# An encoder layer in split precision: weight loads at their place in the program, and the products by sevens one pair later

## The chip, the core and the metric

The kernel runs on one core of one Trainium2 chip. A core has five engines that each work through a list of instructions of their own: TensorE (PE in the profile; its weight loads are PEld), VectorE (DVE), ScalarE (ACT), GpSimd (POOL) and SyncE (SP), which here only sends transfers. They wait for each other by semaphores. Transfers between the main memory and the on-chip memory (SBUF) run on 16 DMA engines. Matmuls write to PSUM, eight banks in all, of which the program uses four as accumulators ("g") and four for other purposes (x, y, sc0, sc1).

The metric is the device time of one execution in microseconds (us), lower is better. The kernel before took 1131.32 us (median of three runs, 1131.21 to 1131.83).

## What is computed

One layer of a bidirectional encoder over 256 tokens of 2048 features: a norm, one projection to nine groups of 2048 columns, two branches (a gated linear recurrence over 16 heads and a short convolution), an output projection over both branches, a gate, and a last norm.

```python
def reference(x, p, norm_w, w_in, ..., w_out, w_ple, w_ple_gate, final_norm_w):
    h = x
    ...
        hn = _rmsnorm(h, norm_w[i])
        proj = hn @ w_in[i]
        q, v, f_fwd, f_bwd, z_a, b_gate, c_gate, h_b, z_b = jnp.split(proj, IN_SPLITS, axis=-1)
        o_a = _hgrn2_bidirectional(jax.nn.silu(q), v, f_fwd, f_bwd, lb_all[:, i])
        o_a = _head_rmsnorm(o_a, hgrn_norm_w[i]) * jax.nn.silu(z_a)
        y_b = b_gate * _short_conv(c_gate * h_b, conv_w[i])
        o_b = _rmsnorm(y_b, conv_norm_w[i]) * jax.nn.silu(z_b)
        h = h + jnp.concatenate([o_a, o_b], axis=-1) @ w_out[i]
        gate = jax.nn.sigmoid(h @ w_ple_gate[i])
        h = h + (p[i] @ w_ple[i]) * gate
    return _rmsnorm(h, final_norm_w)
```

All of it is in float32, and the weights (some 200 MB) are read once.

## The kernel before

**Split precision.** Each float32 operand of the large products is split into a rounded part and the rest. ACT makes the rounded part by a copy (L103, the "cast"), DVE subtracts it from the raw one (L104, the "split"). A product then takes three matmuls: rounded by rounded, rounded by rest, rest by rounded. The activations are split once; the weights are split as they stream in.

**The stream of weights.** The class `Stream` brings the weights in order. A raw tile holds 2048 columns (1 MB) and has three buffers; it is loaded by SP in `load` (L82). It is used in parts of 1024 columns (or less), and each part has one of five split buffers. `get(i)` opens all parts up to three ahead of part i: `open` takes a split buffer, loads the raw tile if it is not there, and returns what `split` works on. In `get` all of this stands under `high_priority(offset=300)`.

**The planner.** The program is written in order, and a planner in the framework sets the order of each engine's list: of the instructions that are ready it takes the one with the lowest number, and numbers follow the order of the program. `high_priority(offset=300)` lowers the number of what stands under it by 300, so that it comes ahead of up to 300 instructions that stand before it. Only the opening stage has an order by hand for ACT, DVE and PE.

**Ticks.** Work that goes beside the products is queued by `at(dt, fn)`: `tick()` is called behind each k-tile of a product, and `fn` is written into the program when `dt` ticks have passed.

**The stages,** with their lines:

- The opening stage, from 0 to about 40 us: x is split (`x_split`, L286 and L287, which read the tile xf), and the first three products (two forget gates and q) run together over k.
- Heads in pairs, four times two pairs. `gemm_in` makes products of 16 k-tiles with four matmuls each (L344, L346), `evac` takes them out of PSUM (L378, L379), `gemm_two` makes v and z for two pairs (L365 to L367). Beside them run the recurrences: `mix_forgets`, `mix_pair`, `scores` (L543, L587), `outputs`.
- The norm of x is needed late, since a row's scale can be multiplied in behind the product. For it the token rows of x are loaded once more into xf, in two transfers (`load_tokens`, L298, ticks 2 and 3 behind the opening stage), squared and summed (`x_squares`, L305 on ACT and L306 on DVE, ticks 6 to 9, into PSUM banks x and y), turned into scales (`x_norms`, L312 to L316, tick 11) and spread by a product (`norms_spread`, L321 and L322, tick 14). `by_norms` (L383) multiplies the forget gates and q by them; the first pair's gates are mixed at tick 15. The first scores are written at tick 18 of the product of v, and their last operand is dd (L515).
- The convolution branch, eight times four products, up to about 844 us. Behind its last product `turn` (L471 to L475) transposes the last two head pairs through PSUM banks y and x into mixa, the input of the output projection. The residual rows hh are loaded by SP (L773).
- The output projection, 845 to about 1019 us: two column halves u, and for each first the recurrence's branch (mixa), then the convolution's (mixb). Each of these four runs of `half` goes over 16 k-tiles in eight pairs. A pair is normally eight products of 128 x 128 by 512 (two k-tiles, two row blocks, two column blocks), 24 matmuls. Two of the pairs are done by seven products, as in Strassen's scheme, 21 matmuls: they need sums of weight blocks, made on DVE in place in the raw tile (`sums`, L69, L71, L72), and sums of activation blocks (`act_sums`, L685 to L690). `SUMS` says which pairs. Their parts are named singles, single, pairs and more, and the last two come behind sums. Four accumulators beside the main four take the products that go to several outputs (epa in banks x, y, sc0, sc1 for mixa, epb in the "g" banks for mixb); they are taken at the first pair of sevens and emptied at the second.
- The gate, the embedding and the last norm, up to the end. The inputs pr and fw are loaded by SP (L910, L915).

Of the kernel before, what the change touches and what calls it, by code (L numbers as in the profile page):

```python
# [12 lines left out]
ALU = mybir.AluOpType  # L13
# [14 lines left out]
class Stream:  # L28
# [11 lines left out]
    def add(self, *srcs):  # L40


        j = len(self.todo)
        _, k, n = srcs[0].shape
        n *= len(srcs)
        self.todo.append((srcs, k, n))
        first = len(self.where)
        self.where += [(j, h) for h in range(k * n // 1024)]
        return list(range(first, len(self.where)))
# [10 lines left out]
    def sums(self, j, h):  # L60

        b = self.raws[j].rearrange("p (b n) -> p b n", b=4)
        add = self.nc.vector.tensor_tensor
        if h == "singles":
            return b[:, 0:2]
        if h == "single":
            return b[:, 3:4]
        if h == "pairs":
            add(out=b[:, 0:3:2], in0=b[:, 0:3:2], in1=b[:, 2:4], op=ALU.add)  # L69
            return b[:, 0:3:2]  # L70
        add(out=b[:, 3], in0=b[:, 0], in1=b[:, 3], op=ALU.add)  # L71
        add(out=b[:, 1], in0=b[:, 3], in1=b[:, 1], op=ALU.add)  # L72
        return b[:, 1:4:2]

    def load(self, j, k0=0, k1=None, pool=None):
# [30 lines left out]
    def get(self, i):  # L106
        while self.next <= min(i + self.ahead, len(self.where) - 1):
            if self.next not in self.parts:

                with self.tc.high_priority(offset=300):  # L110
                    self.split(*self.open(self.next))
            self.next += 1
        return self.parts[i]

# [2 lines left out]
def tile_hymba_encoder(  # L117
# [45 lines left out]
        for c in (B_CG, B_HB, B_BG, B_ZB):  # L163
            blocks[c, i] = sum((ws.add(w_in[c + i, h]) for h in range(2)), [])

    SUMS = (2, 5)
    oblocks = []
    for u in range(2):
        srcs = [[w_out[2 * u + n, q // 2, :, 2 * (q % 2) : 2 * (q % 2) + 2] for n in range(2)] for q in range(16)]
        oblocks.append([(ws.add_sums if q % 8 in SUMS else ws.add)(*srcs[q]) for q in range(16)])  # L170
    gblocks, pblocks = [], []
# [59 lines left out]
    for j in range(4):  # L231
        sgn = 1 if j < 2 else -1
        pool.affine_select(
            out=tri[:, j, :], in_=tri[:, j, :], compare_op=ALU.is_ge, fill=0.0, base=0,
# [447 lines left out]
    def act_sums(src, dst, a, s):  # L682


        dve.tensor_tensor(out=a, in0=src[:, :, 0], in1=src[:, :, 1], op=ALU.add)  # L685
        a11, a21, a12, a22 = (a[:, k, m * P : (m + 1) * P] for k in range(2) for m in range(2))
        for o, x, y in ((0, a21, a22), (1, a21, a11), (2, a11, s[:, 0]), (3, a12, s[:, 2])):
            dve.tensor_tensor(out=s[:, o], in0=x, in1=y, op=ALU.subtract)
        act.copy(out=dst[:, :, 0], in_=s)
        dve.tensor_tensor(out=dst[:, :, 1], in0=s, in1=dst[:, :, 0], op=ALU.subtract)  # L690
# [10 lines left out]
    for i in range(8):  # L701
# [7 lines left out]
        for m in range(2):  # L709
            ct = 2 * i + m  # L710
            dve.tensor_scalar(cg[:, m, :], u[:, m, 0:T], cvw[:, 0, ct : ct + 1], None, op0=ALU.mult)
            for j in (1, 2):
                dve.scalar_tensor_tensor(
                    out=cg[:, m, :], in0=u[:, m, j : j + T], scalar=cvw[:, j, ct : ct + 1],
                    in1=cg[:, m, :], op0=ALU.mult, op1=ALU.add,
# [10 lines left out]
        for m in range(2):  # L726
            ct = 2 * i + m
            dve.scalar_tensor_tensor(
                out=hb[:, m, :], in0=hb[:, m, :], scalar=cnw[:, ct : ct + 1], in1=sz[:, m, :],
# [13 lines left out]
        if i in (4, 5):  # L743
            a = bp.tile([P, 2, T], F32, tag="sa", name=f"sa{i}")
            b = bp.tile([P, 4, P], F32, tag="sb", name=f"sb{i}")
            k = 2 * SUMS[i - 4]
            act_sums(mixa[:, k : k + 2], suma[:, i - 4], a, b)
# [46 lines left out]
    def three(acc, al, ah, w, start, stop):  # L794
# [3 lines left out]
        pe.matmul(acc, lhsT=al, rhs=w[:, 0], start=False, stop=stop)  # L798

    def half(main, extra, parts, src, sums):  # L800


        banks = None
        for q, ids in enumerate(parts):
# [10 lines left out]
            if banks is None:  # L815
                banks = extra()
            z = SUMS.index(q)
            st, sp = z == 0, z == len(SUMS) - 1

# [51 lines left out]
    for u in range(2):  # L871
        cs = [slice(512 * (2 * u + n), 512 * (2 * u + n + 1)) for n in range(2)]
        for src, sums, main, other, scale in ((mixa, suma, psg, psm, False), (mixb, sumb, psm, psg, True)):
            name = f"p{'ab'[scale]}{u}"
            acc = four(main, name)
            parts = oblocks[u][8 * scale : 8 * scale + 8]
            if u == 0 and not scale:
                for z in range(2):
                    k = 2 * SUMS[z]
                    act_sums(  # L880
                        mixb[:, k : k + 2], sumb[:, z], tmp[:, 0:1].rearrange("p b (k t) -> p (b k) t", k=2),
                        tmp[:, 1:2].rearrange("p b (o t) -> p (b o) t", o=4),
                    )
            for q1, q5, q7, q6 in half([acc[0:2], acc[2:4]], lambda: four(other, "e" + name), parts, src, sums):
                d, v, d7, v7 = (tmp[:, b] for b in range(4))
                add_h(0, cs[0], q1, scale)
                act.copy(out=d, in_=q1)
                dve.tensor_tensor(out=d, in0=d, in1=q6, op=ALU.subtract)
                dve.tensor_tensor(out=v, in0=q5, in1=d, op=ALU.subtract)
                dve.tensor_tensor(out=d7, in0=d, in1=q7, op=ALU.subtract)  # L890
                dve.tensor_tensor(out=v7, in0=v, in1=q7, op=ALU.add)
                add_h(0, cs[1], v, scale)
                add_h(1, cs[0], d7, scale)
                add_h(1, cs[1], v7, scale)
            with tc.high_priority(offset=200):
                for m in range(2):
                    for n in range(2):
                        add_h(m, cs[n], acc[2 * m + n], scale)
        for z in range(2):
            at(5 + 2 * z, lambda u=u, z=z: h_transposed(u, z))  # L900
# [161 lines left out]
```

## Time and profile before

| | us |
|---|---|
| median of three runs | 1131.32 |
| the profiled execution | 1129.86 |
| its span, first to last instruction | 1128.1 |
| PE busy | 1113.0 |
| DVE busy | 785.0 |
| ACT busy | 646.9 |

The rest of the page bears on how the transfers stand. The second part cuts the span into 40 slices of 28 us; a digit is a share in tenths.

```profile
DVE  7689467865966587867665566566668888886664
ACT  6688566755865587564454444444545454455563
PEclk9999999999999999999999999999999999999999
DMA  9744455454546545545555555555556575566542
...
q1 hardware_dynamic: 41616, 212.88, 54.9%
```

The DMA engines are near their limit only in the first slice and busy by half later. DVE is busiest in the slices from 840 to 1010 us, those of the output projection. The granted clock of TensorE (PEclk) stands at full speed in all slices at this grain; single dips show only in a finer table.

How the views are read: a row of a timeline gives start, duration, engine, line, operation and tiles, in brackets the idle time before it and who ended it. A row of the list of waits gives the total, the number of times and the longest. A row of groups gives count, total and the mean in ns. A row of the table of stretches gives the busy time and count of PE, PEld, DVE, ACT and POOL, then the granted clock, the share of the DMA engines and GB/s.

### The profile page before, as it was taken

Reading aid. Unit: us, or ns where it says so; the run is one execution under the profiler, and the core shown is the slowest. Engines: PE = TensorE matmul, PEld = TensorE weight load, DVE = VectorE, ACT = ScalarE, POOL = GpSimd, SP = SyncE. Lnnn points to the kernel's source line nnn. Section 1 sums busy time; section 2 is a strip of 40 time slices with the busy share of each in tenths; the row PEclk is TensorE's granted clock in tenths of the full one; section 3 lists DMA queues with packets and bytes.
Section 4 is the critical chain, followed back from the end, with each engine's and each line's share of the span. In section 5 each row is a group of like instructions: output and inputs, shape, how many; then the busy total and the mean of one; then the engine's idle time right before and its main releaser. Section 6 shows DMA issues by size and latency. Waiting matters only on the chain.

```text
span 1128.1 us, 16505 instructions
## 1 busy us (share of the span) xinstructions
PE 1113.0 (99%) x6506; PEld 956.2 (85%) x6506; DVE 785.0 (70%) x1016; ACT 646.9 (57%) x893; POOL 214.4 (19%) x167
## 2 busy tenths in 40 slices
PE   9998999999999999999999999999999999999997
PEld 8887888888888888888888888888887888888886
DVE  7689467865966587867665566566668888886664
ACT  6688566755865587564454444444545454455563
POOL 1035116210432035211111121111211000000012
PEclk9999999999999999999999999999999999999999
DMA  9744455454546545545555555555556575566542
GB/s 351 286 150 170 167 182 192 140 197 167 178 145 220 168 168 187 177 160 196 182 204 195 192 188 187 186 186 187 192 189 216 188 237 172 186 227 234 202 168 75
DMA packets 41981, 214.27 MB, mean 190 GB/s; under 512 B 4656, under 2 KB 5040, under 8 KB 26288
## 3 DMA queue, kind: packets, MB, share of 16 engines
q1 hardware_dynamic: 41616, 212.88, 54.9%
q8 instruction: 51, 0.84, 0.3%
q10 hardware_dynamic: 288, 0.34, 0.1%
q14 instruction: 26, 0.21, 0.1%
HBM read 211.11 MB, written 2.10 MB: 189 GB/s over the span
## 4 chain that ended last, share of the span: by engine, by line
PE 95%; DVE 2%; ACT 1%; POOL 1%; issue 0%; DMA 0%; DVEq 0%; ACTq 0%; POOLq 0%
PE a L346 36%; PE a L344 18%; PE a L367 5%; PE a L366 5%; PE a L365 5%; PE pg L790 3%; PE pg L789 3%; PE pg L791 3%; PE pa L798 2%; PE pa L797 2%; PE pa L796 2%; PE pb_sc L798 1%; PE pb_sc L797 1%; PE pb_sc L796 1%; PE scps L543 1%; DVE spl L104 1%
## 5 line engine op out<-in xcount | busy, mean ns | idle before, releaser
L104 DVE TENSOR_TENSOR spl<-raw,spl 128x1024 fp32r<-128x1024 f32 (+2 forms) x414 | 510.2, 1242 | 250.2 <-ACT spl L103 249.2
L346 PE MATMUL a<-xs,spl 128*128 128x512 f32 x1792 | 620.6, 394 | 0.5 <-DVE xs L287 0.5
L103 ACT CAST spl<-raw 128x1024 fp32r<-128x1024 f32 (+2 forms) x414 | 415.8, 1011 | 313.0 <-PE a L344 171.1
L344 PE MATMUL a<-xs,spl 128*128 128x256 f32 x1792 | 493.3, 278 | 0.0
L346 PEld LDWEIGHTS a<-xs,spl 128*128 128x128 f32 x1792 | 335.0, 188 | 77.5 <-ACT spl L103 0.7
L344 PEld LDWEIGHTS a<-xs,spl 128*128 128x128 f32 x1792 | 335.9, 188 | 1.9
L365 PE MATMUL a<-spl,xs 128*128 128x512 f32 x256 | 100.7, 393 | 0.0
L367 PE MATMUL a<-spl,xs 128*128 128x512 f32 x256 | 99.8, 390 | 0.0
L366 PE MATMUL a<-spl,xs 128*128 128x512 f32 x256 | 99.7, 389 | 0.0
L378 ACT COPY r<-a 128x256 f32<-128x256 f32 x112 | 40.9, 368 | 53.1 <-PE a L344 53.0
L939 POOL TENSOR_TENSOR hh<-hh,fw 128x512 f32<-128x512 f32 (+1 forms) x9 | 11.3, 1263 | 257.5 <-ACT gt L938 254.9
L367 PEld LDWEIGHTS a<-spl,xs 128*128 128x128 f32 x256 | 48.1, 188 | 10.1
L365 PEld LDWEIGHTS a<-spl,xs 128*128 128x128 f32 x256 | 48.1, 188 | 9.6
L366 PEld LDWEIGHTS a<-spl,xs 128*128 128x128 f32 x256 | 48.1, 188 | 9.4
L789 PE MATMUL pg<-spl,ht 128*128 128x512 f32 (+1 forms) x120 | 45.2, 377 | 0.0
L790 PE MATMUL pg<-spl,ht 128*128 128x512 f32 (+1 forms) x120 | 45.1, 375 | 0.0
L791 PE MATMUL pg<-spl,ht 128*128 128x512 f32 (+1 forms) x120 | 45.0, 375 | 0.0
L383 POOL TENSOR_TENSOR xf<-xf,rbc 128x1024 f32<-128x1024 f32 x8 | 20.4, 2556 | 123.1 <-DVE xf L379 117.8
L524 POOL TENSOR_TENSOR qc<-pf,ge 128x256 f32<-128x256 f32 x16 | 32.8, 2051 | 50.2 <-DVE pf L516 29.2
L796 PE MATMUL pa<-spl,mixa 128*128 128x512 f32 x104 | 40.7, 392 | 0.0
L798 PE MATMUL pa<-spl,mixa 128*128 128x512 f32 x104 | 40.5, 389 | 0.0
L797 PE MATMUL pa<-spl,mixa 128*128 128x512 f32 x104 | 40.5, 389 | 0.0
(266 smaller groups left out, 1270.5 us busy)
## 6 DMA issues: line engine op xcount, KB each, us to landing
raw<-in_w_in_dram SPq DMA_DIRECT2D x106, 1024.0 KB, 4.9
raw<-in_w_in_dram SPq DMA_DIRECT2D x74, 512.0 KB, 4.9
raw<-in_w_out_dram SPq DMA_DIRECT2D x64, 512.0 KB, 5.0
raw<-in_w_gate_dram SPq DMA_DIRECT2D x12, 1024.0 KB, 5.0
raw<-in_w_gate_end_dram SPq DMA_DIRECT2D x8, 512.0 KB, 4.9
xf<-in_xtok_dram SPq DMA_DIRECT2D x2, 1024.0 KB, 6.9
hh<-in_xtok_dram SPq DMA_DIRECT2D x1, 2048.0 KB, 11.1
raw<-in_w_ple_dram SPq DMA_DIRECT2D x4, 512.0 KB, 3.6
```

The lines of the kernel that those rows point to most:

```text
L103: self.nc.scalar.copy(out=v[:, :, 0], in_=r)
L104: self.nc.vector.tensor_tensor(out=v[:, :, 1], in0=r, in1=v[:, :, 0], op=ALU.subtract)
L344: pe.matmul(a[:, :T], lhsT=lhsT, rhs=xs[:, kt, 0, :], start=False, stop=(kt == NKT - 1))
L346: pe.matmul(a, lhsT=lhsT, rhs=xs[:, kt, :, :].rearrange("p s n -> p (s n)"), start=(kt == 0), stop=False)
L365: pe.matmul(acc[m], lhsT=lh, rhs=w[:, kt % 2, 0, :], start=(kt == 0), stop=False)
L366: pe.matmul(acc[m], lhsT=lh, rhs=w[:, kt % 2, 1, :], start=False, stop=False)
L367: pe.matmul(acc[m], lhsT=ll, rhs=w[:, kt % 2, 0, :], start=False, stop=(kt == NKT - 1))
L789: pe.matmul(acc[m], lhsT=lh, rhs=wh, start=(kt == 0), stop=False)
L790: pe.matmul(acc[m], lhsT=lh, rhs=wl, start=False, stop=False)
L791: pe.matmul(acc[m], lhsT=ll, rhs=wh, start=False, stop=(kt == nk - 1))
L796: pe.matmul(acc, lhsT=ah, rhs=w[:, 0], start=start, stop=False)
L797: pe.matmul(acc, lhsT=ah, rhs=w[:, 1], start=False, stop=False)
```

## The change

Two edits. First, `get` calls `open`, and with it `load`, before the block of `high_priority`; only the casts and splits stand under it. The sums in `sums`, which `open` calls, get a block of their own with the same offset. So the loads of the weights (and the requests for tiles) take their numbers from where they stand in the program.

Second, `SUMS` goes from (2, 5) to (3, 5): in each run of `half` the fourth and the sixth pair of k-tiles are done by seven products, and no longer the third and the sixth. The weights' order in memory stays; the sums of activation blocks are those of the fourth pair (heads 6 and 7).

```diff
         b = self.raws[j].rearrange("p (b n) -> p b n", b=4)
-        add = self.nc.vector.tensor_tensor
+
+        def add(out, in0, in1):
+            with self.tc.high_priority(offset=300):
+                self.nc.vector.tensor_tensor(out=out, in0=in0, in1=in1, op=ALU.add)
+
         if h == "singles":
             return b[:, 0:2]
         if h == "single":
             return b[:, 3:4]
         if h == "pairs":
-            add(out=b[:, 0:3:2], in0=b[:, 0:3:2], in1=b[:, 2:4], op=ALU.add)
+            add(out=b[:, 0:3:2], in0=b[:, 0:3:2], in1=b[:, 2:4])
             return b[:, 0:3:2]
-        add(out=b[:, 3], in0=b[:, 0], in1=b[:, 3], op=ALU.add)
-        add(out=b[:, 1], in0=b[:, 3], in1=b[:, 1], op=ALU.add)
+        add(out=b[:, 3], in0=b[:, 0], in1=b[:, 3])
+        add(out=b[:, 1], in0=b[:, 3], in1=b[:, 1])
         return b[:, 1:4:2]
...
             if self.next not in self.parts:
+                part = self.open(self.next)
 
                 with self.tc.high_priority(offset=300):
-                    self.split(*self.open(self.next))
+                    self.split(*part)
             self.next += 1
         return self.parts[i]
...
-    SUMS = (2, 5)
+    SUMS = (3, 5)
```

## The prediction

> **What bounds the kernel now.** I read the page's busy shares first, then the list of waits for PE alone, then a table of stretches.
>
> ```profile
> span 1128.1 us, 16505 instructions
> PE 1113.0 (99%) x6506; PEld 956.2 (85%) x6506; DVE 785.0 (70%) x1016; ACT 646.9 (57%) x893; POOL 214.4 (19%) x167
> ...
> PE scps L543 <- DVE dd L515: 2.9, 1, 2.9
> PE epa_x L796 <- DVE mixa L475: 2.3, 1, 2.3
> ...
> 95.00:845.00 750.00, 750.00 (x4700) 651.08 (x4692) 501.79 (x642) 432.19 (x605) 177.73 (x125) 1.00 0.53 181
> 1120.00:1128.10 8.10, 0.00 (x0) 0.00 (x0) 3.23 (x10) 2.77 (x5) 0.72 (x1) 0.74 0.65 243
> ```
>
> PE is idle 1128.1 - 1113.0 = 15.1 us in all. Of this 8.1 us lie behind the last matmul. Two single waits, the longest of the list, make 5.2: 2.9 us before the first scores (L543) and 2.3 us before the first of the seven products (L796 into epa_x). The rest, under 2 us, lies at the very start. Between 95 and 845 us PE has no idle time at all. So a change that leaves the number of matmuls alone can win only at these two places, and it loses only where it makes PE wait anew. This change leaves the number alone: each half still has two pairs of k-tiles with seven products and six with eight. The two places in the timeline of PE, and what DVE did there:
>
> ```profile
> 856.70 0.39 PE L796 MATMUL pa<-spl,mixa 128*128 128x512 f32 x1
> 859.43 0.47 PE L796 MATMUL epa_x<-spl,mixa 128*128 128x512 f32 x1 [2.34 <-DVE mixa L475]
> ...
> 858.81 0.47 DVE L475 SCALAR_TENSOR_TENSOR mixa<-ogt,vec,mixa 128x256 fp32r<-128x256 f32 x1
> ...
> 89.51 0.39 PE L367 MATMUL a<-spl,xs 128*128 128x512 f32 x1
> 89.74 0.39 PE L365 MATMUL a<-spl,xs 128*128 128x512 f32 x1
> 93.04 0.34 PE L543 MATMUL scps<-qc,dd 128*32 128x128 f32 x2 [2.92 <-DVE dd L515]
> 96.80 0.48 PE L366 MATMUL a<-spl,xs 128*128 128x512 f32 x1
> ...
> 114.88 0.30 PE L543 MATMUL scps<-qc,dd 128*32 128x128 f32 x2
> 117.38 0.40 PE L366 MATMUL a<-spl,xs 128*128 128x512 f32 x1
> ...
> 93.50:94.00 0.50, 0.50 (x30) 0.50 (x26) 0.00 (x0) 0.50 (x2) 0.42 (x2) 0.50 0.00 0
> 857.00:859.50 2.50, 0.16 (x2) 0.10 (x1) 2.50 (x7) 2.35 (x4) 0.00 (x0) 1.00 0.00 0
> ```
>
> A matmul of 512 columns normally starts 0.23 us after the one before (89.51, 89.74). The gap 856.70 to 859.43 is 2.73 us, so this wait costs **2.50**. The gap 89.74 to 93.04 is 3.30 us, so that one costs **3.07**. It has an aftermath: behind it the granted clock is 0.50. The same work, from the first scores to the L366 behind them, takes 96.80 - 93.04 = 3.76 us here and 117.38 - 114.88 = 2.50 us in the next group: **1.26** more. Behind the other wait the clock stays at 1.00.
>
> The Trainium skill (TensorE: Matmul & The Clock Gate, Part 1) says that the array falls to half rate after an idle window of about 3.4 us, that this window runs freely, and that it takes as long a busy one to come back. The trace agrees as far as it goes: half clock behind 2.9 idle us, none behind 2.3. By that rule alone, a shorter wait at the scores would cost its own length without the 1.26; this is a rival below.
>
> **The sevens moved from the third to the fourth pair.** epa_x takes the PSUM bank x, which the last transposed head pair still holds until the L475 above has read it, at 859.28. With the third pair done plainly, PE first has 24 more matmuls (two k-tiles, four accumulators, three each): 24 x 0.227 = 5.4 us. It comes to epa_x at about 856.93 + 5.4 = 862.4 instead of 856.93. L475 then has 3 us to spare. DVE does not do more before that point: the third pair's sums and four splits give way to two splits. Even if the last L475 slipped behind two more splits of 1.3 us it would end at 861.9. I take the whole 2.50 as gained; the bounds are 0 and 2.50.
>
> What the move costs is DVE's, since a pair of sevens is cheap for PE and dear for DVE:
>
> ```profile
> L104 DVE TENSOR_TENSOR spl<-raw,spl 128x1024 fp32r<-128x1024 f32 x380 | 489.0, 1295 | 247.4 <-ACT spl L103 246.4
> L104 DVE TENSOR_TENSOR spl<-raw,spl 128x512 fp32r<-128x512 f32 x30 | 19.6, 685 | 2.8 <-ACT spl L103 2.8
> L69 DVE TENSOR_TENSOR raw<-raw 128x1024 f32<-128x1024 f32 x8 | 9.7, 1218 | 0.1
> L72 DVE TENSOR_TENSOR raw<-raw 128x512 f32<-128x512 f32 x8 | 6.2, 777 | 0.2
> L71 DVE TENSOR_TENSOR raw<-raw 128x512 f32<-128x512 f32 x8 | 5.5, 690 | 0.2
> ...
> 918.66 3.51 DVE L104 TENSOR_TENSOR spl<-raw,spl 128x1024 fp32r<-128x1024 f32 x3
> ...
> 921.87 0.39 PE L796 MATMUL pb_x<-spl,mixb 128*128 128x512 f32 x1
> ```
>
> Sevens: 3 x 1.295 + 0.685 + 1.218 + 0.690 + 0.777 = 7.26 us of DVE in 21 x 0.227 = 4.77 us of PE. A plain pair: 2.59 in 5.45. Fourth, fifth and sixth together: DVE 17.1, PE 15.0, so DVE falls 2.1 us behind in each of the four halves, and two plain pairs no longer lie between. What carries it is work made ahead. Five split buffers let DVE run four parts ahead of PE. The tightest part today is the plain one right behind the sevens: its split starts at 918.66 and lasts about 1.2, PE wants it at 921.87, so 2.0 us are left.
>
> I walk through the new order with PE at the first of the fourth pair as 0. The release of the buffer five parts back starts a cast (1.05), and the split (1.22) follows it. The fifth pair's two parts are ready at 2.5 and 3.9, wanted at 4.8 and 7.5. The sixth pair's parts, with its sums between them, are ready at about 5.1, 5.8, 9.6 and 10.8, wanted at 10.2, 11.6, 12.3 and 13.6. The seventh pair's first is ready at 12.8, wanted at 15.0. The least reserve stays near 2 us, so I take 0. If the reserve were not there, the second sevens would run at DVE's pace: 7.26 - 4.77 = 2.5 us in each half, 10 us in all; that is the other bound.
>
> **The weight loads without precedence.** SP sends nothing but loads until the end, and every weight load waits for its raw buffer. Without precedence a load can only lose its place to another load that is ready: the token rows (L298), the residual rows (L773), the two small ones of the last stage. The place where that matters is the start:
>
> ```profile
> 28.19 0.87 DVE L287 SCALAR_TENSOR_TENSOR xs<-xf,vec,xs 128x256 fp32r<-128x256 f32 x2
> ...
> 13.51 27.01 SPq L82 DMA_DIRECT2D raw<-in_w_in_dram  x8
> 40.57 0.42 SPq L298 DMA_DIRECT2D xf<-in_xtok_dram  x1
> 45.85 0.33 SPq L82 DMA_DIRECT2D raw<-in_w_in_dram  x1
> 46.23 0.42 SPq L298 DMA_DIRECT2D xf<-in_xtok_dram  x1
> ...
> 845.06 0.42 SPq L773 DMA_DIRECT2D hh<-in_xtok_dram  x1
> ...
> 42.91 0.42 DVE L379 TENSOR_TENSOR qt<-a,r 128x256 f32<-128x256 f32 x1
> 54.56 0.69 DVE L306 SCALAR_TENSOR_TENSOR xk<-xf 128x512 f32<-128x512 f32 x1
> 65.72 0.42 DVE L322 COPY rbc<-rps 128x256 f32<-128x256 f32 x1
> 91.15 1.75 DVE L515 TENSOR_TENSOR dd<-xf,dd 128x512 f32<-128x512 f32 x1
> ...
> xf<-in_xtok_dram SPq DMA_DIRECT2D x2, 1024.0 KB, 6.9
> ...
> 74.75 0.39 PE L365 MATMUL a<-spl,xs 128*128 128x512 f32 x1
> ```
>
> The token rows overwrite xf, whose last reader ends at 28.19 + 0.87 = 29.06. Yet they are sent at 40.57 and 46.23, each right behind a weight load. In the program they stand at ticks 2 and 3 of the first product behind the opening stage; the weight loads opened at ticks 12 and 20 were sent before the first of them, and that of tick 28 before the second. So the precedence did hold them back. The whole chain to the late scores hangs on the second: sent 46.23, landed about 53.1, squares from 54.56, norms spread at 65.72, last operand of the scores at 91.15 + 1.75 = 92.90.
>
> Without precedence both should go ahead of the loads of ticks 12 to 28, between 29.1 and 41.0. That brings the second 5 to 17 us forward. The gain is capped, because its squares need a PSUM bank that q's accumulator leaves only with the L379 of 42.91: 54.56 to 43.4, 11 us at most. The scores' own place is tick 18 of the product that starts at 74.75: 54 matmuls, 74.75 + 12.3 = 87.0. The operand must be ready by then, 5.9 us sooner than 92.90. With a move of 5 a wait of about 1 us remains, with 11 none. I take none, since the free time of xf (29.06) lies 17 us back: gain 3.07 + 1.26 = **4.33**, bounds 0 and 4.33.
>
> What the moved transfers cost the weights:
>
> ```profile
> 51.99 1.05 ACT L103 CAST spl<-raw 128x1024 fp32r<-128x1024 f32 x1
> ...
> raw<-in_w_in_dram SPq DMA_DIRECT2D x106, 1024.0 KB, 4.9
> ...
> 88.00:90.00 2.00, 2.00 (x10) 1.43 (x8) 2.00 (x5) 1.98 (x2) 1.63 (x2) 1.00 1.00 397
> ```
>
> At 397 GB/s a token load of 1 MB holds the transfers for 2.6 us, both for 5.3. The load sent at 40.2 (last of the eight) lands after 4.9 us and is first cast at 51.99: 6.9 us to spare. So it is hidden. Uncovered, it would cost up to 5.3 us once. The residual rows (845.06) may pass the weight load sent beside them, which is that of the fifth pair; 2 MB are 5.3 us, and PE comes to that pair only four pairs later, over 20 us. The splits and the sums keep their precedence, and the other moved call, the request for the tiles, issues nothing. These I cost at 0, with 5.3 as the bound if the cover were gone.
>
> **The sum.** 2.50 + 4.33 = 6.83 us. The profiled execution took 1129.86 us (span 1128.1), which gives 1123.0. It was 1.46 under the median of the runs, so on the median: 1131.32 - 6.83 = **1124.5**.
>
> **The rivals.**
> (a) *The order of the loads stays.* SP sends the token rows where it did and the scores wait as before: 1131.32 - 2.50 = 1128.8. For it: nothing in the trace shows why SP did not send them soon after 29 us, when they were free to go. Against it: the three weight loads of later ticks that passed them.
> (b) *The wait at the scores shrinks but stays.* The chain comes 5 us forward, or DVE and ACT, both busy nearly all of 60 to 95 us, give part of it back. About 1.5 us are left and the clock holds, as behind 2.3 idle us: 1126.0.
> (c) *The bank wait comes back one pair later.* The last L475 slips behind the splits past 862.4, the scores gain: 1131.32 - 4.33 = 1127.0.
> (d) *DVE becomes the bound around the fifth pair.* This one ends slower. It decides once more than 2 us of other DVE work (squares of sums, transposes, additions to hh) fall into the 15 us from the fourth to the sixth pair: then each half pays up to 2.5, 1124.5 + 10 = 1134.5. For it: DVE is busy 25 of 27 us in the first half. Against it: that other work has no precedence and can be late.
> (e) *Neither wait goes*: 1131.3.
>
> ```profile
> 863.00:890.00 27.00, 27.00 (x121) 22.37 (x120) 25.19 (x33) 14.04 (x15) 0.00 (x0) 1.00 0.69 237
> ```
>
> **How the numbers follow.** Forecast 0.40, (a) 0.22, (b) 0.15, (c) 0.06, (d) 0.11, (e) 0.06. About 0.2%, 2.26 us, is what a measurement of this kernel can tell from no change. The forecast, (b) and (c) lie clearly beyond it; (a) is 0.22% and falls beyond it in 0.14 of its 0.22. Faster 0.40 + 0.15 + 0.06 + 0.14 = 0.75, same 0.08 + 0.06 = 0.14, slower 0.11. The range reaches from 1123.0 (the sum on the profiled execution itself) to 1129.5 (case (a) with the 0.6 us by which the three runs differ), and leaves out (d) and (e), 0.17.
>
> **What would show it.** Right: the list of waits for PE keeps only the two at the start; L298 is sent before 41 us and rbc copied before 61; the granted clock stays 1.00 from 90 to 97; DVE's last L475 ends before epa_x starts. Wrong: L298 still behind the same weight loads; a wait of PE on a split between the fourth and seventh pair of any half; a cast in 35 to 60 us that waits for a weight transfer.

## The result, and the profile after

| | before | after |
|---|---|---|
| median, us | 1131.26 (1130.22 to 1131.83, 4 runs) | 1122.49 (1121.94 to 1123.00, 4 runs) |
| profiled execution, us | 1129.86 | 1121.94 |
| its span, us | 1128.1 | 1120.2 |

The ratio is 0.9923, with a 95% interval of 0.9906 to 0.9941: faster by 8.8 us. The forecast was 1124.5 with a range from 1123.0 to 1129.5. The sign and both places were right; the time lies 0.5 us below the range.

In the kernel after, lines from L82 on stand four to five lower: the load is L86, cast and split L107 and L108, `load_tokens` L303, the scores L548, `turn`'s last operation L480, the products by sevens L801 to L803, and all sums of weight blocks L66.

The page of after, and the list of waits for PE:

```profile
span 1120.2 us, 16504 instructions
PE 1110.8 (99%) x6506; PEld 955.9 (85%) x6506; DVE 788.6 (70%) x1016; ACT 644.7 (58%) x892; POOL 216.5 (19%) x167
...
PE wps L221 <- DVE wz L216: 1.1, 1, 1.1
```

PE makes the same 6506 matmuls. Its two long waits are gone from the list, and no new one has come; only the opening one is left. DVE has the same 1016 operations. The work is the same; only idle time of PE, and half-clock time behind it, went.

SP's own timeline of after shows how the first wait went (transfers of one line that follow each other are one row, with their count at its end):

```profile
19.94 9.30 SPq L303 DMA_DIRECT2D xf<-in_xtok_dram  x2
29.28 94.90 SPq L86 DMA_DIRECT2D raw<-in_w_in_dram  x25
```

The two token loads, sent at 40.57 and 46.23 before, now stand one behind the other, and the next weight load is behind both. The group begins at 19.94 and ends at 29.24 (19.94 + 9.30). The first load fills the half of xf that was read first; SP sent the second at 28.91, as soon as the last reader of the other half had ended (28.87 in DVE's timeline). From there the timelines of DVE and PE of after show the chain to the scores and, further down, the bank x:

```profile
41.20 0.70 DVE L311 SCALAR_TENSOR_TENSOR xk<-xf 128x512 f32<-128x512 f32 x1
52.30 0.42 DVE L327 COPY rbc<-rps 128x256 f32<-128x256 f32 x1
79.68 0.68 DVE L520 TENSOR_TENSOR dd<-xf,dd 128x512 f32<-128x512 f32 x1
846.34 0.48 DVE L480 SCALAR_TENSOR_TENSOR mixa<-ogt,vec,mixa 128x256 fp32r<-128x256 f32 x1
...
85.99 0.39 PE L372 MATMUL a<-spl,xs 128*128 128x512 f32 x1
86.31 0.30 PE L548 MATMUL scps<-qc,dd 128*32 128x128 f32 x2
88.50 0.47 PE L370 MATMUL a<-spl,xs 128*128 128x512 f32 x1
856.77 0.39 PE L801 MATMUL epa_x<-spl,mixa 128*128 128x512 f32 x1
```

The squares began at 41.20 instead of 54.56, 13.4 us sooner, the scale was spread at 52.30 instead of 65.72, and the last operand of the scores, dd, was ready at 80.36 instead of 92.90. The scores then start 0.32 us behind the matmul before them, with 5.9 us to spare. Likewise the last L480 ended at 846.82, 9.9 us before epa_x wants its bank.

The table of stretches of after, in the places of the old waits (the third number from the end is the granted clock):

```profile
91.00:94.00 3.00, 3.00 (x15) 2.49 (x14) 3.00 (x5) 1.56 (x2) 1.15 (x2) 1.00 0.59 213
94.00:97.00 3.00, 3.00 (x15) 2.46 (x15) 3.00 (x9) 1.61 (x3) 0.00 (x0) 1.00 0.00 0
858.00:861.00 3.00, 3.00 (x15) 2.50 (x14) 2.97 (x7) 2.69 (x5) 0.00 (x0) 1.00 0.81 268
```

PE is busy throughout, at full clock.

**Where the 7.95 us of span went.** Both kernels make 6506 matmuls, so the starts of matmuls with the same number can be compared. Counted from the first matmul and cut at the matmuls 270 (about 49 us), 1000 (about 163) and 4950 (about 795, ahead of the output projection), the traces give:

| stretch | before | after | difference |
|---|---|---|---|
| to matmul 270: opening stage | 48.56 | 48.04 | -0.52 |
| 270 to 1000: holds the first scores | 113.81 | 108.98 | -4.83 |
| 1000 to 4950 | 631.04 | 631.04 | 0.00 |
| 4950 to the last: holds epa_x | 325.09 | 322.49 | -2.60 |

The rest behind the last matmul is the same. Some 630 us in the middle agree to the hundredth, so nothing is paid back there. What must be explained is the two stretches with the waits, and the half microsecond of the opening.

### The profile page after: what moved, and what is told of

The parts are those of the page before. It is cut to its first block, busy times and chain, and to the rows that moved or that the text cites. A ratio compares the mean times of both kernels' runs of the same rounds, so it can differ in the third digit from the quotient of the medians.

```text
span 1120.2 us, 16504 instructions
## 1 busy us (share of the span) xinstructions
PE 1110.8 (99%) x6506; PEld 955.9 (85%) x6506; DVE 788.6 (70%) x1016; ACT 644.7 (58%) x892; POOL 216.5 (19%) x167
## 4 chain that ended last, share of the span: by engine, by line
PE 99%; ACT 0%; DVE 0%; DVEq 0%; issue 0%; ACTq 0%
PE a L351 37%; PE a L349 19%; PE a L372 5%; PE a L370 5%; PE a L371 5%; PE pg L794 3%; PE pg L796 3%; PE pg L795 3%; PE pa L801 2%; PE pa L803 2%; PE pa L802 2%; PE pb_sc L801 1%; PE pb_sc L803 1%; PE pb_sc L802 1%; PE scps L548 1%; PE cx L592 1%
## 5 line engine op out<-in xcount | busy, mean ns | idle before, releaser
L108 DVE TENSOR_TENSOR spl<-raw,spl 128x1024 fp32r<-128x1024 f32 (+2 forms) x414 | 512.7, 1248 | 243.8 <-ACT spl L107 242.6
L107 ACT CAST spl<-raw 128x1024 fp32r<-128x1024 f32 (+2 forms) x414 | 415.1, 1011 | 307.0 <-PE a L349 162.2
L801 PE MATMUL pa<-spl,mixa 128*128 128x512 f32 x104 | 40.7, 392 | 0.0
L803 PE MATMUL pa<-spl,mixa 128*128 128x512 f32 x104 | 40.5, 390 | 0.0
```

The lines of the kernel that those rows point to most:

```text
L107: self.nc.scalar.copy(out=v[:, :, 0], in_=r)
L108: self.nc.vector.tensor_tensor(out=v[:, :, 1], in0=r, in1=v[:, :, 0], op=ALU.subtract)
L801: pe.matmul(acc, lhsT=ah, rhs=w[:, 0], start=start, stop=False)
```

## The experiments

The theory is the prediction's: two separate waits, one for each edit; the loads' edit works through the token loads alone, the sums' edit through the place of epa_x. Two rivals: the edits act together (the loads' order moves the splits, and with them L480), or it is the weight loads, not the token loads, that gain from the first edit.

**One edit at a time.** The sums alone, on the kernel before:

```diff
-    SUMS = (2, 5)
+    SUMS = (3, 5)
```

> Only SUMS = (3, 5); the loads keep their precedence. If the two waits are independent (my reading): the wait of epa_x goes, 2.5 us, so a ratio near 0.9978; the wait before the first scores stays at about 3 us with the half clock behind it. If the missing 1 to 2 us of the prediction belong to this edit: 3.5 to 4.5 us, 0.996 to 0.997.

Measured: 1127.88 us (1126.19 to 1128.13, 6 runs), ratio to before 0.9968 (0.9957 to 0.9980). PE's list:

```profile
PE scps L543 <- DVE dd L515: 2.9, 1, 2.9
...
```

The loads alone, on the kernel after:

```diff
-    SUMS = (3, 5)
+    SUMS = (2, 5)
```

> Only the loads without precedence; SUMS = (2, 5). Independent waits: 4.3 us less, ratio near 0.9962, the wait of epa_x stays at 2 to 3 us. If the faster pace of the first 52 us (0.347 us for a pair of matmuls instead of 0.353) comes from the order of the transfers: 5.5 to 6 us, 0.995, and the pace is 0.347 here and 0.353 in the run with the sums alone.

Measured: 1125.58 us (1124.76 to 1126.46, 5 runs), ratio 0.9953 (0.9939 to 0.9966). PE's list:

```profile
PE epa_x L801 <- DVE mixa L480: 2.4, 1, 2.4
...
```

Each edit takes exactly one wait away and leaves the other at its length. Beside before's 1130.85 in the same comparison the two are worth 2.97 and 5.27, together 8.24; both at once gave 8.77 and, in a repeat below, 7.98. They add up within the scatter of the medians, and more sharply in the traces: the sums alone shorten the stretch of epa_x by 2.57 us (322.52), the loads alone that of the scores by 4.83 (108.98), and both edits give 2.60 and 4.83. The edits do not act together.

The other theory on record for the loads, that the order of the transfers sets the pace of the first 52 us, fails: a pair of matmuls starts every 0.347 us in both of these profiles.

**The token loads alone.** In the kernel before only these two transfers get the precedence too; all weight loads keep theirs:

```diff
     def load_tokens(m):
-        nc.sync.dma_start(xf32[...], xtok[:, m])
+        with tc.high_priority(offset=300):
+            nc.sync.dma_start(xf32[...], xtok[:, m])
```

> The kernel before, with the two token loads under the same precedence as the weight loads, and nothing else. If the whole effect of the first edit is that the token rows are sent earlier: the same time as with the loads without precedence, within 0.1%. If the loads' own numbers matter beside it (the order of casts, splits or later loads): a part of it only, at least 1 us apart.

Measured: 1125.55 us (1125.18 to 1127.82, 5 runs), ratio 0.9956 (0.9943 to 0.9969), the same as the loads' edit. SP's timeline and PE's list of this kernel:

```profile
19.36 8.83 SPq L299 DMA_DIRECT2D xf<-in_xtok_dram  x2
28.24 96.89 SPq L82 DMA_DIRECT2D raw<-in_w_in_dram  x25
...
PE epa_x L797 <- DVE mixa L476: 2.3, 1, 2.3
```

The order of the transfers is that of after, and the stretch with the scores takes 108.94 us, beside 108.98 in both kernels with the loads' edit. So the whole gain of the first edit comes from two transfers of 1 MB that go ahead; the weights are not better served by it. The pace of the first 52 us was 0.353 here, with the same order of transfers.

**The kernels themselves again.** Before:

> The kernel before once more, for its profile. If the pace of the first 52 us belongs to the execution and not to the kernel, it may be 0.347 us here; if it belongs to the kernel before, 0.353 us again. The waits at the scores (2.9) and at epa_x (2.3) come again within 0.3 us in both cases.

One execution took 1129.45 us, with waits of 2.9 and 2.4 us (2.9 and 2.3 in the first profile) and stretches of 113.95 and 325.13. From 12 us on its pace was 0.347, so the pace belongs to the execution and not to the kernel. After:

> The changed kernel once more, for a tighter interval and a second profile. From the second profile on, the two waits account for 6.8 to 7.1 us (4.2 to 4.4 at the scores with the clock behind them, 2.6 at epa_x). If that is all, the medians differ by about 7 and the rest of the 8.8 first measured was scatter of the opening stage; if something else gains, they differ by 8 to 9 again and a stretch of the profile other than these two and the first 52 us is shorter.

Measured: 1122.71 us (1122.20 to 1123.41, 5 runs) beside 1130.69 of before, ratio 0.9930 (0.9917 to 0.9942); stretches of 109.13 and 322.47. The difference of the medians, 7.98, lies at the edge of the second case, but no third stretch is shorter: the middle takes 631.04 us in both second profiles. The two stretches are 4.82 and 2.66 us shorter, 7.48 together, more than the 6.8 to 7.1 expected of the waits; the other 0.5 is within what one kernel's executions differ by.

**The sums at other pairs.** How much room the sums' edit has on both sides, tried on the kernel after. With the second pair:

```diff
-    SUMS = (3, 5)
+    SUMS = (1, 5)
```

> The changed kernel with SUMS = (1, 5): the first sevens one pair earlier than in the kernel before, two earlier than in the changed one. If epa_x waits for the bank that the transposed heads hold: PE comes to it 10.9 us sooner, the wait is 5 us or more, over 3.4 us, so the clock falls to 0.50 behind it and costs up to 1.7 us more; 6 to 12 us above the changed kernel. If the wait came from DVE being behind with the sums: it is about as long as at (2, 5), 2 to 3 us, since the sums move with it.

Measured: 1123.79 us (1123.31 to 1124.27, 5 runs), ratio to before 0.9939 (0.9925 to 0.9953). This was a miss: epa_x came one pair earlier than in the kernel that waits, and yet hardly waited. DVE's timeline and PE's list of this kernel, and behind them DVE's of the kernel with the loads' edit alone, where the third pair has the sums:

```profile
842.53 0.87 DVE L480 SCALAR_TENSOR_TENSOR mixa<-ogt,vec,mixa 128x256 fp32r<-128x256 f32 x2
...
843.93 0.47 DVE L480 SCALAR_TENSOR_TENSOR mixa<-ogt,vec,mixa 128x256 fp32r<-128x256 f32 x1
...
846.77 0.48 DVE L480 SCALAR_TENSOR_TENSOR mixa<-ogt,vec,mixa 128x256 fp32r<-128x256 f32 x1
...
PE epa_x L801 <- DVE mixa L480: 0.2, 1, 0.2
```

```profile
843.42 0.48 DVE L480 SCALAR_TENSOR_TENSOR mixa<-ogt,vec,mixa 128x256 fp32r<-128x256 f32 x1
845.35 0.48 DVE L733 SCALAR_TENSOR_TENSOR hb<-hb,vec,szb 128x256 f32<-128x256 f32 x1 [1.46 <-ACT szb L730]
845.86 0.69 DVE L108 TENSOR_TENSOR spl<-raw,spl 128x512 fp32r<-128x512 f32 x1
...
846.87 0.69 DVE L66 TENSOR_TENSOR raw<-raw 128x512 f32<-128x512 f32 x1
847.47 0.48 DVE L480 SCALAR_TENSOR_TENSOR mixa<-ogt,vec,mixa 128x256 fp32r<-128x256 f32 x1
847.86 1.39 DVE L66 TENSOR_TENSOR raw<-raw 128x512 f32<-128x512 f32 x1
...
850.34 1.23 DVE L108 TENSOR_TENSOR spl<-raw,spl 128x1024 fp32r<-128x1024 f32 x1 [0.26 <-ACT spl L107]
851.48 0.48 DVE L480 SCALAR_TENSOR_TENSOR mixa<-ogt,vec,mixa 128x256 fp32r<-128x256 f32 x1
...
852.55 1.22 DVE L108 TENSOR_TENSOR spl<-raw,spl 128x1024 fp32r<-128x1024 f32 x1
853.68 0.48 DVE L480 SCALAR_TENSOR_TENSOR mixa<-ogt,vec,mixa 128x256 fp32r<-128x256 f32 x1
```

The four L480 that read the banks are the point. With the third pair's sums (L66) and splits among them they stretch from 843.42 to 854.16; with the sums at the second or the fourth pair they are done by 847.25 and 846.82. So the old wait did not come from epa_x being early. Between the first L480 and the end of the last stand two sums of the third pair (2.1 us) and three of its splits (3.1), which have precedence; DVE also waited 1.5 us there for ACT (L733), which is not work of that pair. What epa_x waited for was an operation that its own pair's sums and splits had pushed back. The runs move sums and splits together, so they do not show what each is worth alone. This kernel lost 0.9 us in the stretch of epa_x (323.35 beside 322.47), 0.35 of it at epa_x itself (846.82 to 847.40, where 0.23 is normal).

With the fifth pair, so that two pairs of sevens stand side by side:

```diff
-    SUMS = (3, 5)
+    SUMS = (4, 5)
```

> The changed kernel with SUMS = (4, 5): no plain pair between the two by sevens. Walked through with the same durations, the second group's sums are ready 0.8 us after PE wants them and the part behind by as much, so about 1 us in each of four halves, 3 to 6 us above the changed kernel, with waits of PE on the split of sums. If DVE's reserve is larger than I reckoned: within 0.1% of the changed kernel and no wait of PE.

Measured: 1123.52 us (1122.88 to 1124.27, 5 runs), ratio 0.9937 (0.9924 to 0.9949): 0.8 us above the kernel after in the same comparison, less than expected. PE's list names no wait, but in the timelines of PE and of DVE the sixth pair of the last half shows small ones:

```profile
1000.25 0.40 PE L801 MATMUL epb<-spl,sumb 128*128 128x512 f32 x1
1000.55 0.50 PE L802 MATMUL pb_sc<-spl,mixb 128*128 128x512 f32 x1
1000.89 0.39 PE L803 MATMUL pb_sc<-spl,mixb 128*128 128x512 f32 x1
...
999.28 3.49 DVE L108 TENSOR_TENSOR spl<-raw,spl 128x1024 fp32r<-128x1024 f32 x3
```

Matmuls that start every 0.23 us stand 0.30 and 0.34 apart there: the first of the three splits from 999.28 on lasts 1.22 us, to 1000.50, and is needed then. The two late parts of a half and the part behind them take about 0.26 us more, in all four halves: 1.0 us, and the stretch is 1.0 longer (323.47). The reserve of DVE is just used up; the backlog of adjacent sevens is real, but little of it reaches PE. Neither place beats the fourth pair. For the fourth and seventh pair, SUMS = (3, 6), which would leave two plain pairs between the sevens, there is no measured time, so whether it is faster stays open.

**Why before's executions differ.** Before's profiled execution lay 1.46 us under its median, after's 0.55 under its own. To see what differs, the kernel before ran four times more with a profile.

> The kernel before, unchanged, once more, to see where its executions differ (the profiled ones took 1129.45 and 1129.86 us, the median of the others 1130.7). Theory 1, the opening stage: the matmuls of the first 52 us start every 0.3467 or 0.3535 us, pair by pair, and nothing else differs; the stretch with the first scores takes 76.0 to 76.2 us and the one with epa_x 325.1 again, and an execution over 1130.5 us is late already at the first product. Theory 2, the clock: the half-clock time behind the two waits is longer in some executions, so the stretch with the scores grows to 77.5 or more, or the granted clock falls behind epa_x too and its stretch takes 326.5 or more.

The other three carried the same two theories. The stretches of the table are those of the section on the result, cut at other matmuls than in the expectation. In the table, the time of each profiled execution of before (the first two are those above), its three stretches, when TensorE's clock first rose, and when it fell to half later on:

| us | to matmul 270 | scores | epa_x | clock rose | half clock |
|---|---|---|---|---|---|
| 1129.86 | 48.56 | 113.81 | 325.09 | 4.38 | 93.12 to 96.54 |
| 1129.45 | 47.95 | 113.95 | 325.13 | 4.11 | 92.86 to 96.27 |
| 1130.20 | 48.85 | 113.80 | 325.11 | 4.59 | 93.34 to 96.75 |
| 1131.57 | 49.14 | 113.26 | 326.71 | 6.50 | 859.83 to 863.24 |
| 1130.06 | 48.80 | 113.73 | 325.10 | 4.41 | 93.16 to 96.57 |
| 1130.54 | 49.03 | 113.99 | 325.11 | 5.20 | 93.95 to 97.36 |

Both theories hold a part. Among the five with the same clock the opening makes up 1.08 of the 1.09 us between the lowest and the highest. The slowest lost 1.6 us more at epa_x, where its clock fell, and kept full clock at the scores. There it gained only 0.55 us by that (113.26 beside 113.81): at full clock PE meets further small waits behind the scores, which the list of this execution names and those of the others do not:

```profile
PE cx L587 <- POOL kx L530: 0.5, 2, 0.3
```

The table of stretches of that execution, and of the first one of before in the same places:

```profile
91.00:94.00 3.00, 0.35 (x24) 0.38 (x28) 2.82 (x3) 2.97 (x5) 2.37 (x2) 1.00 0.40 153
94.00:97.00 3.00, 2.80 (x85) 2.34 (x74) 1.80 (x3) 2.97 (x4) 1.35 (x2) 1.00 0.00 0
...
858.00:861.00 3.00, 1.53 (x5) 1.23 (x5) 2.97 (x10) 2.78 (x4) 0.00 (x0) 0.80 0.24 72
861.00:864.00 3.00, 3.00 (x10) 2.39 (x9) 2.38 (x3) 2.06 (x2) 0.00 (x0) 0.63 0.77 272
```

```profile
91.00:94.00 3.00, 0.96 (x36) 0.99 (x40) 2.22 (x3) 2.99 (x5) 2.29 (x3) 0.85 0.26 105
94.00:97.00 3.00, 3.00 (x63) 2.94 (x56) 2.40 (x4) 2.48 (x3) 1.24 (x2) 0.58 0.08 14
...
858.00:861.00 3.00, 1.57 (x7) 1.34 (x8) 2.97 (x10) 2.82 (x5) 0.00 (x0) 1.00 0.37 81
861.00:864.00 3.00, 3.00 (x15) 2.49 (x14) 3.00 (x3) 2.96 (x3) 0.00 (x0) 1.00 0.76 269
```

The waits are the same in both; the clock falls behind the one or the other.

## Why the prediction was right in part, and where it failed

**The bound of the kernel, and the two places.** Right. PE had no other idle time to give, the stretch from 163 to 795 us did not change, and each edit alone took away the wait that was put to it.

**The weight loads without precedence.** The order and the chain came as worked out: both token loads before 29.3 us, the squares at 41.20 (43.4 had been put as the earliest, for the bank that q's accumulator leaves; DVE emptied that bank by 41.17 here, so the cap lay 2 us earlier, and the squares began right behind it), dd ready 5.9 us before the scores. No cost of the moved transfers shows: the list of PE names no wait for a weight. The token run shows that nothing else in this edit counts. The size was short. The scores were put at 3.07 + 1.26 = 4.33, and the stretch gave 4.83. The wait itself is right: the gap ahead of the scores fell from 3.30 to 0.32 us, 2.98. The aftermath was mis-sized, and the half clock is not all of it. The 1.26 came from comparing the first scores with the next group, 2.50 us. In the kernel after, the same first scores take 88.50 - 86.31 = 2.19 us, 1.57 less than the 3.76 of before. But the one execution of before that kept full clock there (1131.57) still took 2.75 (93.65 to 96.40), and its whole stretch 113.26 us, 4.28 more than after's 108.98. So by this one execution the half clock accounts for only 0.55 of the 4.83; with the clock at full, PE met other short waits that the kernel after does not have. What is left of the 4.83 beside 2.98 and 1.57, 0.3 us, lies in steps too small to name.

**The sevens one pair later.** The 2.50 was right in size (2.60), and the sentence that DVE does not do more before that point was true but said too little: DVE does less, and the last L480 came at 846.82 and not near 859. The working gave epa_x 3 us of cover by its later place; the second-pair run shows that it was enough for nearly all of it that the pair's sums and extra splits left.

**DVE's reserve.** Put at about 2 us in the tightest part. Between split and matmul it is 2.0 us or more in three of the halves, but less in the first: DVE's and PE's timelines of after

```profile
864.00 0.69 DVE L695 TENSOR_TENSOR sumb<-tmp,sumb 128x512 fp32r<-128x512 f32 x1
...
865.29 1.23 DVE L108 TENSOR_TENSOR spl<-raw,spl 128x1024 fp32r<-128x1024 f32 x1
866.43 0.68 DVE L66 TENSOR_TENSOR raw<-raw 128x512 f32<-128x512 f32 x1
868.31 2.36 DVE L108 TENSOR_TENSOR spl<-raw,spl 128x1024 fp32r<-128x1024 f32 x2 [1.19 <-ACT spl L107]
...
870.37 0.39 PE L801 MATMUL pa<-spl,mixa 128*128 128x512 f32 x1
```

show the last part of the sixth pair split by 868.31 + 1.22 = 869.53 and wanted at 870.37: 0.84 us left, where one sum of activation blocks (L695) stands between the weights' sums and the third of these (866.43) comes behind a split; in the other halves the three follow one another. Rival (d) named the right mechanism and came within a microsecond of it. The adjacent-pairs run, where it bites, shows that the price is not the full lag of 2.5 us a half but 0.26; that work made ahead in the split buffers carries the rest is argued, not shown.

**The step that failed** is the way from the sum to the median, and the range that was built on it, with the aftermath's term mis-sized on top. The two terms were 6.83 together; the two stretches gave 7.43. The text took 6.83 from the profiled execution (1123.0) and made this the low end, as if no gain could be larger than the two terms as sized. With the terms as measured, 1129.86 - 7.43 = 1122.43 would just have held 1122.49. For the forecast it then added the 1.46 by which the profiled execution lay under its median, as if after's had to lie as far under its own; it lies 0.55 under.

So the forecast of 1124.5 misses the 1122.49 by 2.0 us: 0.6 by the two terms (0.50 and 0.10), 0.5 by the opening, and 0.9 by the offset (1.46 against 0.55). The half microsecond of the opening is not shown to come from the change: to matmul 270 the seven profiles with the late token loads took 47.95 to 49.14 us, the six with the early ones 48.04 to 49.01. The offset of 1.46 fits the scatter of before, its opening (up to 1.2 us between executions) and the clock at epa_x (1.6 in one of six), but the three executions behind that median have no profile, so what they spent it on is not shown. After has no wait long enough for the clock to fall at, and its nine runs in two comparisons lie within 1.5 us, where the 23 of before in three span 3.6.

**The rivals.** (a), (b), (c) and (e) fell with the list of waits, which names neither place any more; (d) is weighed above.

## What to carry to other kernels

When PE is busy 99% of the span, look for the single long waits, and ask of each what stood in front of its releaser on the releaser's own queue: here weight loads with too much precedence stood before two token loads, and a pair's own sums and splits before the operation that frees its bank. Precedence belongs on the work that is late, not on a whole call that issues transfers as well. And before a gain of under 1% is forecast to the microsecond, take several profiles of the unchanged kernel: one execution is one draw of the opening and of the clock.

## What the runs showed of the hardware that was not expected

**The clock goes by the phase of a window.** In every execution the time between two changes of the granted clock ahead of the last matmul is a multiple of 3.413 us: 88.75 us (26 times) from the first rise to the fall at the scores, 853.33 (250 times) to the fall at epa_x, and each half-clock spell lasts 3.41. Laid on that grid, the windows of the waits that held 2.3 to 2.9 idle us were followed by half clock, all seven of them (before six times, the sums alone once), and those with 1.9 or less never. A wait of 2.8 to 2.9 us lost the clock where it fell into one window and kept it where it was cut into 1.0 and 1.8 (the execution of 1131.57); the wait of 2.3 at epa_x, usually cut, lost it there. The prediction's reading, half clock behind 2.9 and none behind 2.3, was a matter of phase. The Trainium skill (TensorE: Matmul & The Clock Gate, Part 1) gives a free-running window of 3413 ns, and the trace agrees to the nanosecond; but it speaks of an idle window, and here some 70% of idle time in a window was enough.

**PE has two paces at the start.** The pairs of one matmul of 256 and one of 512 columns start every 0.3467 us, but from about 9 to 50 us of many executions every 0.3533, 1.9% slower at a granted clock of 1.00. In the stretch from 9 to 49 us the first profiles of before and of after show

```profile
9.00:49.00 40.00, 40.00 (x229) 34.77 (x229) 30.60 (x56) 26.68 (x49) 0.00 (x0) 1.00 0.87 337
```

```profile
9.00:49.00 40.00, 40.00 (x232) 35.31 (x232) 32.26 (x67) 30.09 (x57) 1.47 (x3) 1.00 0.88 350
```

that is 229 matmuls and 232. Five of the six profiles of before have the slower pace (the repeat ran at the faster one from 12 us on). Both profiles of after have the faster, as have the sums alone and the loads alone; the token run and the sums at the second and at the fifth pair have the slower. So it follows neither edit. What sets it stayed open.
